# A hybrid layer in fp32: more groups of the two FFNs by seven products, sums of weights held in the program's place, loads asked for sooner

## The chip, the cores and the metric

One core of a Trainium2 chip runs the whole layer. The time is the device time of one execution in microseconds; the kernel before was run three times. Its five instruction streams are TensorE (PE; its weight loads are listed as PEld), VectorE (DVE), ScalarE (ACT), GpSimd (POOL) and SyncE (SP), which only issues DMAs here.

## The reference

One layer, 256 rows of 2048 numbers, all fp32, d_ff = 5632:

```python
x = x + 0.5 * swiglu(rms_norm(x, ffn1_norm), ffn1_w_gate, ffn1_w_up, ffn1_w_down)
h = rms_norm(x, mix_norm)
proj = h @ w_in                                   # u | q | k | v
y_ssm = s5_mixer(u, ...)                          # complex diagonal recurrence, chunks of 64, then GLU
y_sb = stick_breaking_attention(q, k, v)
mixed = concat(rms_norm(y_ssm), rms_norm(y_sb))
x = x + mixed @ w_out
x = x + 0.5 * swiglu(rms_norm(x, ffn2_norm), ffn2_w_gate, ffn2_w_up, ffn2_w_down)
x = x + rms_norm((p @ w_ple_proj) * sigmoid(rms_norm(x, ple_norm) @ w_ple_gate))

def swiglu(h, w_gate, w_up, w_down):
    return (silu(h @ w_gate) * (h @ w_up)) @ w_down
```

## The kernel before

Every fp32 product is made of three matmuls with a reduced type (fp32r): an operand is split into a high part (`whi` of a weight, by ScalarE, L168) and a low part (`wlo = w - whi`, by VectorE, L171), and high times high, high times low and low times high are added up in PSUM. Activations lie as stationary tiles of 128 x 128 (`nhi`, `nlo`, in the second FFN also `hhi`, `hlo`), weights move, 512 columns a matmul. A tile of weights is 128 x 1024, two of 128 rows.

Gate and up of an FFN are computed in NF = 11 blocks of 512 columns. The inner dimension of 2048 is cut into 4 groups of 512 rows (1 MB of weights each). A plain group has 4 halves (two of gate, two of up), each of 12 matmuls of 128x512 (`gemm_half`, L286, L287, L291): 48 in all. A half needs one `whi` and one `wlo`.

A group can also be done by seven products (`pair`; a scheme of Strassen's kind over gate and up together): the four quarters of weights of gate (`dg`) and up (`du`) and of activations are added and subtracted first, and seven products of 6 matmuls (`product`, L301, L305) take the place of the 48: 42 matmuls. The sums of weights are three `t` a group (L480, VectorE) and one more that a DMA adds in place (POOL's queue). The sums of activations (`shi`, `slo`) are made once by `quarter_sums` and kept. Behind the products of the first four kinds, four merges on VectorE (L516, L520, L523, L524; names `joined`, `left_over`, `parted`) and two copies on ScalarE move what is in one accumulator to the next; then the last three kinds of products are added. The remaining groups are plain (`rest`). In before the first FFN does two groups of blocks 7 to 10 in this way, the second two groups of blocks 1 to 10: 28 groups. With two groups there are 14 products: a0, a1, z0, z1, y0, y1, x0, x1, a'0, a'1, y'0, y'1, x'0, x'1 in the program's order.

When a block's up is complete, VectorE multiplies it with silu of gate (two instructions, `h`, L556 in a pair and L596 elsewhere), then turns the result for the down projection (`mid`, L203, 32 x 32 transpositions) and DMAs write it out (`hidden`). Then comes the next block's first product.

While the first FFN runs, the recurrence's constants are prepared in small pieces (`prep`, lines 860 to 990): a list `beside` holds generators, and `step()` advances each of them by one piece between halves of matmuls. The loads and sums of a pair (`fetch`), the delayed works (`put_off`) and the preparation are all such generators. The buffers of the pairs take the place of the preparation's, so the preparation has to be finished before the first pair's loads: `early = 6` in before.

The order on each engine: instructions that the program pins (`pin`) keep the program's order; the others are placed by a planner, by their costs and by what they need. Each engine then takes its instructions in the order laid down. Buffers that set the pace: four `whi`, four `wlo`, three `raw` (weights of 1 MB as loaded), four accumulators and two others (`aux`) in PSUM.

The norm ahead of an FFN (`Normed`) turns each block of 512 columns either on VectorE with 16 DMAs behind it (on a queue that is given), or, for the last blocks (`late`), by eight transposes on TensorE (L389).

Of the kernel before, what the change touches and what calls it, by code (L numbers as in the profile page):

```python
# [33 lines left out]
def layer_kernel(ctx: ExitStack, tc: tile.TileContext, a: dict, shapes: dict, out: bass.AP):  # L34
# [273 lines left out]

    def quarter_sums(pool, part):

        hi, lo = part
        full, s = (com("h").rearrange("p (j t) -> p j t", t=T), com("h").rearrange("p (i j t) -> p i j t", i=4, j=2))
        nc.vector.tensor_tensor(out=full, in0=hi.bitcast(F32), in1=lo.bitcast(F32), op=ALU.add)
        a11, a12, a21 = (full[:, 2 * k : 2 * k + 2, t * P : (t + 1) * P] for t, k in ((0, 0), (0, 1), (1, 0)))
        a22 = full[:, 2:, P:]
        for o, x, y, op in (
            (0, a21, a22, ALU.subtract), (1, s[:, 0], a11, ALU.subtract), (2, a11, a21, ALU.subtract),
            (3, a12, s[:, 1], ALU.add),
        ):
            nc.vector.tensor_tensor(out=s[:, o], in0=x, in1=y, op=op)  # L320
        shi, slo = (pool.tile([P, 4, 2, P], F32R, name=uid(n)) for n in ("shi", "slo"))
        split(shi, slo, s)
        quarters = [
            tuple(u[:, 2 * k : 2 * k + 2, t * P : (t + 1) * P] for u in part) for t, k in ((0, 0), (0, 1), (1, 1))
        ]
        return quarters, [(shi[:, i], slo[:, i]) for i in range(4)]

# [96 lines left out]

    def ffn(i, xn, nxt, bg=None):
        wg, wu, wd = (a[f"ffn{i}_w_{s}"][0] for s in ("gate", "up", "down"))
        hT = []
        pools = ExitStack()
        early = 6 if bg else NF
        hp = pools.enter_context(phase(f"h{i}"))  # L430
# [16 lines left out]

        first_pair = (early if bg else 0) + 1
        spare = "h" if bg else "n"
        left, right, sums, early_acts = [], {}, {}, {}  # L450
        n_groups = 2

        def fetch(f, steps=2):


            def g():
                todo = []
                for i in range(n_groups):
                    left_, right_ = (
                        get(hp, f"{s}{i}", 4 * NB).rearrange("p (j n) -> p j n", j=4) for s in ("dg", "du")  # L460
                    )
                    for d, w in ((left_, wg), (right_, wu)):
                        rows = w[i * NB : (i + 1) * NB, f * NB : (f + 1) * NB]
                        nc.sync.dma_start(d, rows.rearrange("(j p) n -> p j n", p=P))
                    t1, t2, t4 = (
                        (
                            actp.tile([P, 1024], F32, tag=spare + home, name=uid("t"), bufs={"n": 4, "h": 2}[spare])
                            if home
                            else get(hp, f"t{i}")
                        ).rearrange("p (j n) -> p j n", j=2)  # L470
                        for home in ("hi", "lo", "")
                    )
# [26 lines left out]

        def rest(ps, w, f):  # L500
            for k0 in range(4 * n_groups, KD, 4):
                part = xn(k0 // 4)
                for half in list(weight_halves(w, k0, 4, f * NB)):
                    end = k0 + 4 == KD and half[0] == 1
                    gemm_half(ps, (part, half), range(TT), False, end, skip_group_check=True)
                    step()

        def pair(f, prefetch):

            a, x, z, y = (acc() for _ in range(4))  # L510
            groups = [(*left[i], right.pop((f, i))) for i in range(n_groups)]
            c, u2 = get(hp, "c"), get(hp, "u2", NB)
            c1, c5 = c[:, :NB], c[:, NB:]

            def joined():
                nc.vector.tensor_tensor(out=u2, in0=z, in1=c1, op=ALU.add)  # L516

            def left_over():
                nc.scalar.copy(c5, y)
                nc.vector.tensor_tensor(out=y, in0=y, in1=u2, op=ALU.subtract)  # L520

            def parted():
                nc.vector.tensor_tensor(out=x, in0=x, in1=u2, op=ALU.add)  # L523
                nc.vector.tensor_tensor(out=z, in0=c5, in1=x, op=ALU.subtract)  # L524
# [10 lines left out]
            for i in range(len(todo)):  # L535
# [16 lines left out]
            rest([y, z], wu, f)  # L552
            hh = com("h")
# [5 lines left out]
            put_off(2, turned, hp, f, hh)  # L559

        for f in range(NF):
            if prep and f == min(early, NF - 1):
                finish(prep)
                side.close()
                prep = None
                hp = pools.enter_context(phase(f"h{i}b"))
            if f >= first_pair:
# [20 lines left out]
            if f + 1 == first_pair:  # L588
                left += [quarter_sums(hp, xn(i)) for i in range(n_groups)]
                fetch(f + 1, 1)  # L590
            pu = gemm_block(xn, wu, f * NB, KD)
# [13 lines left out]
    def down(w, hT, nxt, early_acts):  # L605
# [47 lines left out]
        def right(pool, g, n0):  # L653
# [9 lines left out]
            def g_():  # L663
                yield
                yield
                nc.vector.tensor_tensor(out=t, in0=b[2], in1=b[0], op=ALU.subtract)
                yield
# [117 lines left out]
    def s5_prep(pools):  # L785
# [82 lines left out]
        def cmul(o, x, mr, mi, shape, conj=False):  # L868
# [5 lines left out]
            for v, (u, m) in zip(tv, ((x[0], mrb), (x[1], mib), (x[1], mrb), (x[0], mib))):  # L874
                tt(out=v, in0=u, in1=m, op=ALU.mult)
            tt(out=o[0], in0=tv[0], in1=tv[1], op=ALU.add if conj else ALU.subtract)
# [52 lines left out]
        for q in range(NQ):  # L929
            r8 = slice(8 * q, 8 * q + 8)  # L930
# [3 lines left out]
            nc.scalar.dma_start(ceq[:, : 2 * P], a["ssm_c_laid"][:, q * 2 * P : (q + 1) * 2 * P])  # L934
            yield
# [11 lines left out]
            for i in range(2):  # L947
# [3 lines left out]
                for g in range(2):  # L951
                    sl = slice(64 * g, 64 * g + 64)
                    nc.scalar.copy(vv[sl, :, :, g, :], dvv[sl, :, i, :, :])
                    for b in range(2):
                        cv = cb[i][b].rearrange("p (r k g h) -> p k r g h", r=4, k=SL + 1, g=2)
                        nc.scalar.copy(cv[sl, :, :, g, :], cev[sl, :, i, 4 * b : 4 * b + 4, :])
            yield
            for i, n in enumerate(("m1r", "m1i")):
# [26 lines left out]
            mv = m3.rearrange("p (b r c) -> p b r c", b=2, r=4)  # L985
            for r in range(4):
                for sidx in range(SL):
                    o = mv[32 * sidx : 32 * sidx + 32, :, r, 32 * sidx :]
                    i = pv[32 * r : 32 * r + 32, :, : P - 32 * sidx]
                    nc.scalar.copy(o, i)  # L990
            nc.scalar.dma_start(scr["m3"][q], m3)
            yield


# [351 lines left out]

    n1, nm, n2, npl = Normed("ffn1_norm", load_turned), Normed("mix_norm"), Normed("ffn2_norm", kinds="hhnn", late=2), Normed("ple_norm")
    ffn(1, n1, nm, s5_prep)
# [31 lines left out]
    w_out = a["w_out"][0]  # L1380
    for n, side in ((0, 0), (1, 0), (0, 1), (1, 1), (2, 0), (2, 1), (3, 0), (3, 1)):
# [6 lines left out]
        if side:  # L1388
            put_off(2, n2.block, n)
    atp.close()  # L1390
    mix.close()

    ffn(2, n2, npl)


# [159 lines left out]
```

## Time and profile before

| | |
|---|---|
| Median of three runs (lowest, highest) | 1862.11 us (1862.07, 1864.48) |
| The profiled execution, its span | 1862.27 us, 1860.5 us |
| Granted TensorE clock | 0.999 |
| TensorE busy, VectorE, ScalarE, GpSimd | 99%, 80%, 59%, 4% |
| Mean DMA rate | 237 GB/s |

A profile row has the time of the start (in the timeline), the busy time, the engine, the line of the kernel, the operation, and the tile written and those read. What stands in brackets is the idle time of the engine just ahead and what ended it. In a table of stretches the columns are the stretch, its length, the busy time of PE, PEld, DVE, ACT and POOL with the number of instructions, the granted clock, the DMA engines' share and GB/s. In a list of waits: engine, tile and line that waited, what it waited for, us in total, times, the longest. A matmul's duration overlaps that of the next; the distance of two starts tells what one costs.

### The profile page before, as it was taken

Reading aid. Unit: us, or ns where it says so; the run is one execution under the profiler, and the core shown is the slowest. Engines: PE = TensorE matmul, PEld = TensorE weight load, DVE = VectorE, ACT = ScalarE, POOL = GpSimd, SP = SyncE. Lnnn points to the kernel's source line nnn. Section 1 sums busy time; section 2 is a strip of 40 time slices with the busy share of each in tenths; the row PEclk is TensorE's granted clock in tenths of the full one; section 3 lists DMA queues with packets and bytes.
Section 4 is the critical chain, followed back from the end, with each engine's and each line's share of the span. In section 5 each row is a group of like instructions: output and inputs, shape, how many; then the busy total and the mean of one; then the engine's idle time right before and its main releaser. Section 6 shows DMA issues by size and latency. Waiting matters only on the chain. (4 is left out here: it accounts for less than half of the span.)

```text
span 1860.5 us, 24329 instructions
## 1 busy us (share of the span) xinstructions
PE 1846.4 (99%) x8914; PEld 1522.4 (82%) x8914; DVE 1481.4 (80%) x1954; ACT 1103.6 (59%) x1343; POOL 72.2 (4%) x108
## 2 busy tenths in 40 slices
PE   9999999999999999999999999999999999999998
PEld 7888887888887888888898888888888888788886
DVE  8995767899877988686556879999889987798755
ACT  7456665566555665455785656556566655466654
POOL 0000000000000002010010000000000000000100
PEclk9999999999999999999999999999999999999999
DMA  8787779666888768675547757878677688775753
GB/s 320 228 263 248 260 248 308 232 226 215 290 255 279 222 199 304 226 259 184 204 137 242 255 153 246 269 239 264 215 243 227 224 296 262 258 240 194 233 198 125
DMA packets 272793, 441.40 MB, mean 237 GB/s; under 512 B 18208, under 2 KB 89120, under 8 KB 272544
## 3 DMA queue, kind: packets, MB, share of 16 engines
q1 hardware_dynamic: 254992, 409.06, 65.3%
q0 software_dynamic: 5056, 15.73, 4.2%
q10 hardware_dynamic: 12624, 15.04, 2.3%
q8 instruction: 70, 1.15, 0.3%
q14 instruction: 51, 0.42, 0.1%
HBM read 393.64 MB, written 26.21 MB: 226 GB/s over the span
## 5 line engine op out<-in xcount | busy, mean ns | idle before, releaser
L168 ACT CAST whi<-raw 128x1024 fp32r<-128x1024 f32 x514 | 535.8, 1052 | 467.4 <-PE acc L287 321.1
L171 DVE TENSOR_TENSOR wlo<-raw,whi 128x1024 fp32r<-128x1024 f32 x514 | 620.5, 1224 | 220.8 <-ACT whi L168 218.9
L286 PE MATMUL acc<-whi,nhi 128*128 128x512 f32 x1440 | 565.1, 392 | 2.5 <-ACT whi L168 2.3
L287 PE MATMUL acc<-whi,nlo 128*128 128x512 f32 x1440 | 561.2, 390 | 0.0
L291 PE MATMUL acc<-wlo,nhi 128*128 128x512 f32 x1440 | 386.4, 389 | 0.0
L286 PEld LDWEIGHTS acc<-whi,nhi 128*128 128x128 f32 x1440 | 270.6, 188 | 62.3 <-ACT whi L168 3.6
L291 PEld LDWEIGHTS acc<-wlo,nhi 128*128 128x128 f32 x1440 | 270.3, 188 | 56.4
L287 PEld LDWEIGHTS acc<-whi,nlo 128*128 128x128 f32 x1440 | 270.7, 188 | 55.1
L286 PE MATMUL acc<-whi,hhi 128*128 128x512 f32 x576 | 225.3, 391 | 0.0
L287 PE MATMUL acc<-whi,hlo 128*128 128x512 f32 x576 | 224.6, 390 | 0.0
L168 ACT CAST whi<-t 128x1024 fp32r<-128x1024 f32 x114 | 120.0, 1053 | 91.9 <-PE acc L287 52.2
L171 DVE TENSOR_TENSOR wlo<-t,whi 128x1024 fp32r<-128x1024 f32 x114 | 135.4, 1219 | 27.6 <-ACT whi L168 27.6
L291 PE MATMUL acc<-wlo,hhi 128*128 128x512 f32 x576 | 154.4, 390 | 2.9 <-DVE wlo L171 2.9
L291 PEld LDWEIGHTS acc<-wlo,hhi 128*128 128x128 f32 x576 | 107.8, 188 | 26.8 <-DVE wlo L171 4.6
L286 PEld LDWEIGHTS acc<-whi,hhi 128*128 128x128 f32 x576 | 108.2, 188 | 24.2
L287 PEld LDWEIGHTS acc<-whi,hlo 128*128 128x128 f32 x576 | 108.1, 188 | 23.2
L301 PE MATMUL acc<-whi,shi 128*128 128x512 f32 x224 | 89.2, 398 | 0.0
L301 PE MATMUL acc<-whi,slo 128*128 128x512 f32 x224 | 88.0, 393 | 0.0
L168 ACT CAST whi<-dg 128x1024 fp32r<-128x1024 f32 x56 | 58.6, 1050 | 30.4 <-PE acc L287 19.0
L171 DVE TENSOR_TENSOR wlo<-dg,whi 128x1024 fp32r<-128x1024 f32 x56 | 67.5, 1209 | 11.0 <-ACT whi L168 10.6
L305 PE MATMUL acc<-wlo,shi 128*128 128x512 f32 x224 | 70.4, 395 | 0.0
L171 DVE TENSOR_TENSOR wlo<-du,whi 128x1024 fp32r<-128x1024 f32 x56 | 67.6, 1207 | 0.0
(320 smaller groups left out, 2092.7 us busy)
## 6 DMA issues: line engine op xcount, KB each, us to landing
raw<-in_ffn_w_down SPq DMA_DIRECT2D x68, 1024.0 KB, 7.0
raw<-in_ffn_w_up SPq DMA_DIRECT2D x60, 1024.0 KB, 7.0
raw<-in_ffn_w_gate SPq DMA_DIRECT2D x58, 1024.0 KB, 7.3
raw<-in_w_in SPq DMA_DIRECT2D x32, 1024.0 KB, 5.6
dg<-in_ffn_w_gate SPq DMA_DIRECT2D x28, 1024.0 KB, 7.1
du<-in_ffn_w_up SPq DMA_DIRECT2D x28, 1024.0 KB, 8.9
hf<-hidden SPq DMA_DIRECT2D x44, 512.0 KB, 5.7
raw<-in_w_out SPq DMA_DIRECT2D x16, 1024.0 KB, 5.5
```

Of the source, the lines that this page charges most:

```text
L168: copy = nc.scalar.copy(hi, src)
L171: nc.vector.tensor_tensor(out=lo, in0=src, in1=hi.bitcast(F32), op=ALU.subtract)
L286: nc.tensor.matmul(ps[t], lhsT=lh, rhs=hi[:, j, cols], start=t in starts and j == 0, stop=False, **kw)
L287: nc.tensor.matmul(ps[t], lhsT=ll, rhs=hi[:, j, cols], start=False, stop=False, **kw)
L291: nc.tensor.matmul(ps[t], lhsT=lh, rhs=lo[:, j, cols], start=False, stop=stop and j == 1, **kw)
L301: nc.tensor.matmul(ps, lhsT=l[:, j], rhs=hi[:, j], start=start and i + j == 0, stop=False, skip_group_check=True)
L305: nc.tensor.matmul(ps, lhsT=ahi[:, j], rhs=lo[:, j], start=False, stop=j == 1, skip_group_check=True)
```

## The change

It does eight things.

1. `first_pair` of the first FFN is 4 instead of 7, with one group in blocks 4 to 7 and two in 8 to 10; of the second it is 0 instead of 1, with one group in block 0. 31 groups instead of 28.
2. The preparation ends at block 7 (`early = 7`) and is held while products run (`step(prep)`); 16 copies at the end of each of its stages become a generator of their own (`placed`), and its inputs are loaded a stage sooner (`inputs`).
3. The loads for the first pair (`fetch`) are spread (`gap=2`) and begin earlier.
4. The sums of weights are pinned (L487), and so is the addition of high and low parts in `quarter_sums` (L313) and a product in the preparation.
5. `u2` goes, its value being put in the place of `c1`.
6. `quarter_sums` works in place, and the sums of group 1 are made a block before they are needed.
7. The second FFN's norm turns all four blocks on VectorE (`late=0`), the third block's 16 DMAs on SP's queue, the fourth's on POOL's. The last four steps of the projection ahead of it are handed in as `lead`, so that the first pair's loads and sums go between them.
8. In block 0 of the second FFN the groups 1 and 2 of gate and of up come first, then group 3 of both.

On VectorE the program now has in block 3 of the second FFN the first of the following pieces in place of the second. `wlo` is a low part, `h` the product of silu and up of the block before, `t`, `tlo`, `thi` are sums of weights, `dg` and `du` weights as loaded. Of the change:

```order
L487 TENSOR_TENSOR tlo_1788_10284<-thi_1787_10283,du_1786_10280 128x1024
L487 TENSOR_TENSOR t_1784_10278<-tlo_1783_10277,dg_1780_10272 128x1024
L171 TENSOR_TENSOR wlo_10435<-dg_1780_10272,whi_10434 128x1024
L570 SCALAR_TENSOR_TENSOR h_10426<-acc_10098,sm_9491,sg_10334 128x512
L570 SCALAR_TENSOR_TENSOR h_10426<-acc_10099,sm_9491,sg_10334 128x512
L171 TENSOR_TENSOR wlo_10439<-dg_1785_10279,whi_10438 128x1024
L171 TENSOR_TENSOR wlo_10443<-tlo_1783_10277,whi_10442 128x1024
L171 TENSOR_TENSOR wlo_10453<-tlo_1788_10284,whi_10452 128x1024
L487 TENSOR_TENSOR t_1789_10285<-tlo_1788_10284,dg_1785_10279 128x1024
L171 TENSOR_TENSOR wlo_10465<-thi_1782_10276,whi_10464 128x1024
L171 TENSOR_TENSOR wlo_10475<-thi_1787_10283,whi_10474 128x1024
L523 TENSOR_TENSOR c_10433<-acc_10431,c_10433 128x512
```

Of before:

```order
L480 TENSOR_TENSOR t_1766_10206<-t_10205,dg_1762_10200 128x1024
L171 TENSOR_TENSOR wlo_10306<-raw_10303,whi_10305 128x1024
L171 TENSOR_TENSOR wlo_10310<-raw_10303,whi_10309 128x1024
L171 TENSOR_TENSOR wlo_10357<-dg_1757_10193,whi_10356 128x1024
L171 TENSOR_TENSOR wlo_10361<-dg_1762_10200,whi_10360 128x1024
L171 TENSOR_TENSOR wlo_10365<-t_10198,whi_10364 128x1024
L556 SCALAR_TENSOR_TENSOR h_10347<-acc_10019,sm_9456,sg_10255 128x512
L556 SCALAR_TENSOR_TENSOR h_10347<-acc_10018,sm_9456,sg_10255 128x512
L171 TENSOR_TENSOR wlo_10375<-t_10205,whi_10374 128x1024
L171 TENSOR_TENSOR wlo_10387<-t_10197,whi_10386 128x1024
L171 TENSOR_TENSOR wlo_10397<-t_10204,whi_10396 128x1024
```

Three low parts of the pair stood ahead of `h`, now one; all six sums stood ahead, now one stands behind three low parts. The same holds for blocks 5, 7 and 9. In blocks 2, 4, 6, 8, 10 of the second FFN, and 10 of the first, three low parts stay ahead and one sum comes behind `h`; in block 9 of the first two stay ahead; blocks 8 of the first and 1 of the second are as before.

On TensorE the second half of the same pair's products now reads as follows (`acc_10429` is a and a', `acc_10430` x, `acc_10432` y):

```order
L301 MATMUL acc_10430<-whi_10495,slo_9516 128x512
L305 MATMUL acc_10430<-wlo_10496,shi_9515 128x512 x2
L301 MATMUL acc_10432<-whi_10532,shi_9297 128x512
L301 MATMUL acc_10432<-whi_10532,slo_9298 128x512
L301 MATMUL acc_10432<-whi_10532,shi_9297 128x512
L301 MATMUL acc_10432<-whi_10532,slo_9298 128x512
L305 MATMUL acc_10429<-wlo_10511,hhi_9217 128x512 x2
L301 MATMUL acc_10429<-whi_10520,hhi_9325 128x512
...
L305 MATMUL acc_10429<-wlo_10521,hhi_9325 128x512 x2
L305 MATMUL acc_10432<-wlo_10533,shi_9297 128x512 x2
```

The low matmuls of the ninth product (`wlo_10511`) come behind its own four high ones, the rest of the eighth product and the high ones of y'; in before each product's six matmuls stand together.

On SP's queue the first pair's loads now stand among the plain loads of an earlier block:

```order
 L275 DMA raw_583<-in_ffn_w_gate 128x4x512
 L275 DMA raw_658<-in_ffn_w_gate 128x4x512
+L469 DMA dg_227_1520<-in_ffn_w_gate 128x4x512
 L275 DMA raw_719<-in_ffn_w_gate 128x4x512
 L133 DMA h_559<-in_not_ahead 128x128
+L469 DMA du_228_1521<-in_ffn_w_up 128x4x512
 L275 DMA raw_844<-in_ffn_w_up 128x4x512
 L275 DMA raw_923<-in_ffn_w_up 128x4x512
```

Two loads, each with a plain load behind it; in before four stood together.

The diff, cut to its core:

```diff
-    def step():
+    def step(but=None):
         for g in list(beside):
-            if next(g, beside) is beside:
+            if g is not but and next(g, beside) is beside:
...
-    def quarter_sums(pool, part):
+    def quarter_sums(pool, part, tag="h"):
...
+        full = com(tag).rearrange("p (j t) -> p j t", t=T)
+        pin(nc.vector.tensor_tensor(out=full, in0=hi.bitcast(F32), in1=lo.bitcast(F32), op=ALU.add))
...
-    def ffn(i, xn, nxt, bg=None):
+    def ffn(i, xn, nxt, bg=None, lead=()):
...
-        early = 6 if bg else NF
+        early = 7 if bg else NF
...
-        first_pair = (early if bg else 0) + 1
+        first_pair = 4 if bg else 0
+        homes = [hp, hp]
-        n_groups = 2
-        def fetch(f, steps=2):
+        def n_groups(f):
+            return 2 if f > (early if bg else 0) else 1
+        def fetch(f, steps=2, gap=0):
...
                         nc.sync.dma_start(d, rows.rearrange("(j p) n -> p j n", p=P))
+                        for _ in range(gap):
+                            yield
...
                     yield
-                    nc.vector.tensor_tensor(out=o, in0=x, in1=y, op=ALU.add)
+                    pin(nc.vector.tensor_tensor(out=o, in0=x, in1=y, op=ALU.add))
...
             def joined():
-                nc.vector.tensor_tensor(out=u2, in0=z, in1=c1, op=ALU.add)
+                nc.vector.tensor_tensor(out=c1, in0=z, in1=c1, op=ALU.add)
...
                 if i % 2 or i + 1 == len(todo):
-                    step()
+                    step(prep)
             finish(sums.pop(f))
...
-            rest([a, x], wg, f)
+            left_over_groups = list(range(n_groups(f), ND))
+            if len(left) < n_groups(f + 1):
+                left.append(quarter_sums(homes[1], xn(1), "sg"))
+            if f == 0:
+                rest([a, x], wg, f, left_over_groups[:-1])
+                rest([y, z], wu, f, left_over_groups[:-1])
+                del left_over_groups[:-1]
+            rest([a, x], wg, f, left_over_groups)
...
+        for n, block in enumerate(lead):
+            if n == 0:
+                fetch(0, 4, 2)
+            if n == len(lead) - 1:
+                left.append(quarter_sums(hp, xn(0), "sg"))
+            block()
...
+            if f + 1 == first_pair:
+                fetch(f + 1, 2, 2)
...
+            def placed(q=q, pv=pv, mv=mv):
+                for r in range(4):
+                    for sidx in range(SL):
...
+                        pin(nc.scalar.copy(o, i))
+                    yield
+                nc.scalar.dma_start(scr["m3"][q], m3)
+            last = start(placed())
...
-    n2 = Normed("ffn2_norm", kinds="hhnn", late=2)
+    n2 = Normed("ffn2_norm", kinds="hhnn", late=0)
...
+        if side and n == ND - 1:
+            put_off(0, n2.block, n, (1, 9), nc.gpsimd)
+        elif side:
+            put_off(1, n2.block, n, (3, 10), nc.sync)
...
+    blocks = [lambda n=n, side=side: project(n, side) for n in range(2, ND) for side in range(2)]
+    ffn(2, n2, npl, lead=blocks)
```

More of the change, by code (lines that the diff above doesn't have):

```diff
@@ L307, in product, with quarter @@
         return run
-    def quarter_sums(pool, part):
+    def quarter_sums(pool, part, tag="h"):
         hi, lo = part
[L312 to L315, printed above, removed]
+        full = com(tag).rearrange("p (j t) -> p j t", t=T)
+        pin(nc.vector.tensor_tensor(out=full, in0=hi.bitcast(F32), in1=lo.bitcast(F32), op=ALU.add))
+        def quarter(u, t, k):
+            return u[:, 2 * k : 2 * k + 2, t * P : (t + 1) * P]
+        a11, a12, a21, a22 = (quarter(full, t, k) for t in range(2) for k in range(2))
         for o, x, y, op in (
-            (0, a21, a22, ALU.subtract), (1, s[:, 0], a11, ALU.subtract), (2, a11, a21, ALU.subtract),
-            (3, a12, s[:, 1], ALU.add),
-        ):
[L320 to L326, printed above, removed]
+            (a22, a21, a22, ALU.subtract), (a21, a11, a21, ALU.subtract), (a11, a22, a11, ALU.subtract),
+            (a12, a12, a11, ALU.add),
+        ):
+            nc.vector.tensor_tensor(out=o, in0=x, in1=y, op=op)
+        sums = tuple(pool.tile([P, 4, T], F32R, name=uid(n)) for n in ("shi", "slo"))
+        split(*sums, full)
+        return (
+            [tuple(quarter(u, t, k) for u in part) for t, k in ((0, 0), (0, 1), (1, 1))],
+            [tuple(quarter(u, t, k) for u in sums) for t, k in ((1, 1), (0, 0), (1, 0), (0, 1))],
+        )
     def gemm_block(act, w, n0, nkt, first=()):
@@ L464, in g @@
                         nc.sync.dma_start(d, rows.rearrange("(j p) n -> p j n", p=P))
+                        for _ in range(gap):
+                            yield
                     t1, t2, t4 = (
                         (
-                            actp.tile([P, 1024], F32, tag=spare + home, name=uid("t"), bufs={"n": 4, "h": 2}[spare])
-                            if home
-                            else get(hp, f"t{i}")
+                            actp.tile([P, 1024], F32, tag="h" + home, name=uid("t"), bufs=2)
+                            if bg and home
+                            else get(homes[i], f"t{home}{i}")
                         ).rearrange("p (j n) -> p j n", j=2)
@@ L498, in begin_down, with rest @@
             put_off(5, halved)
[L500 to L504, printed above, removed]
+        def rest(ps, w, f, groups):
+            for g in groups:
+                part = xn(g)
+                for half in list(weight_halves(w, 4 * g, 4, f * NB)):
+                    end = g == ND - 1 and half[0] == 1
                     gemm_half(ps, (part, half), range(TT), False, end, skip_group_check=True)
@@ L510, in pair @@
             a, x, z, y = (acc() for _ in range(4))
-            groups = [(*left[i], right.pop((f, i))) for i in range(n_groups)]
-            c, u2 = get(hp, "c"), get(hp, "u2", NB)
+            groups = [(*left[i], right.pop((f, i))) for i in range(n_groups(f))]
+            c = get(hp, "c")
             c1, c5 = c[:, :NB], c[:, NB:]
             def joined():
-                nc.vector.tensor_tensor(out=u2, in0=z, in1=c1, op=ALU.add)
+                nc.vector.tensor_tensor(out=c1, in0=z, in1=c1, op=ALU.add)
             def left_over():
                 nc.scalar.copy(c5, y)
-                nc.vector.tensor_tensor(out=y, in0=y, in1=u2, op=ALU.subtract)
+                nc.vector.tensor_tensor(out=y, in0=y, in1=c1, op=ALU.subtract)
             def parted():
-                nc.vector.tensor_tensor(out=x, in0=x, in1=u2, op=ALU.add)
+                nc.vector.tensor_tensor(out=x, in0=x, in1=c1, op=ALU.add)
                 nc.vector.tensor_tensor(out=z, in0=c5, in1=x, op=ALU.subtract)
@@ L588, in ffn @@
             if f + 1 == first_pair:
-                left += [quarter_sums(hp, xn(i)) for i in range(n_groups)]
-                fetch(f + 1, 1)
+                left.append(quarter_sums(hp, xn(0)))
             pu = gemm_block(xn, wu, f * NB, KD)
@@ L663, in g_ @@
             def g_():
-                yield
-                yield
-                nc.vector.tensor_tensor(out=t, in0=b[2], in1=b[0], op=ALU.subtract)
+                for _ in range(4):
+                    yield
+                pin(nc.vector.tensor_tensor(out=t, in0=b[2], in1=b[0], op=ALU.subtract))
                 yield
@@ L927, in view, with inputs @@
             return [u[:, (2 * k + i) * P : (2 * k + i + 1) * P].rearrange("p (r h) -> p r h", h=HC) for i in range(2)]
-        for q in range(NQ):
-            r8 = slice(8 * q, 8 * q + 8)
+        def inputs(q):
             dv = get(sub, "dv")
@@ L934, in s5_prep @@
             nc.scalar.dma_start(ceq[:, : 2 * P], a["ssm_c_laid"][:, q * 2 * P : (q + 1) * 2 * P])
+            return dv
+        nxt_dv = inputs(0)
+        for q in range(NQ):
+            r8 = slice(8 * q, 8 * q + 8)
+            dv = nxt_dv
             yield
@@ L956, in s5_prep @@
                         nc.scalar.copy(cv[sl, :, :, g, :], cev[sl, :, i, 4 * b : 4 * b + 4, :])
+            if q + 1 < NQ:
+                nxt_dv = inputs(q + 1)
             yield
@@ L985, in s5_prep @@
             mv = m3.rearrange("p (b r c) -> p b r c", b=2, r=4)
[L986 to L991, printed above, removed]
+            def placed(q=q, pv=pv, mv=mv):
+                for r in range(4):
+                    for sidx in range(SL):
+                        o = mv[32 * sidx : 32 * sidx + 32, :, r, 32 * sidx :]
+                        i = pv[32 * r : 32 * r + 32, :, : P - 32 * sidx]
+                        pin(nc.scalar.copy(o, i))
+                    yield
+                nc.scalar.dma_start(scr["m3"][q], m3)
+            last = start(placed())
             yield
+        finish(last)
     ua = [None, None]
@@ L1380, in layer_kernel, with project @@
     w_out = a["w_out"][0]
-    for n, side in ((0, 0), (1, 0), (0, 1), (1, 1), (2, 0), (2, 1), (3, 0), (3, 1)):
+    def project(n, side):
         y, r = ((yss, rss), (ysb, rsb))[side]
@@ L1387, in layer_kernel @@
             )
-        if side:
-            put_off(2, n2.block, n)
+        if side and n == ND - 1:
+            put_off(0, n2.block, n, (1, 9), nc.gpsimd)
+        elif side:
+            put_off(1, n2.block, n, (3, 10), nc.sync)
+    for n, side in ((0, 0), (1, 0), (0, 1), (1, 1)):
+        project(n, side)
     atp.close()
     mix.close()
-    ffn(2, n2, npl)
+    blocks = [lambda n=n, side=side: project(n, side) for n in range(2, ND) for side in range(2)]
+    ffn(2, n2, npl, lead=blocks)
     fin = ctx.enter_context(phase("ple"))
```

13 lines of the change are left out of this document (6 added, 7 removed).

## The prediction

> **What bounds the kernel now.** I read the page's first part first, then the groups by line, then the waits, and last the order of time around the blocks that change.
>
> ```profile
> PE 1846.4 (99%) x8914; PEld 1522.4 (82%) x8914; DVE 1481.4 (80%) x1954; ACT 1103.6 (59%) x1343; POOL 72.2 (4%) x108
> PE acc L291 <- DVE wlo L171: 2.9, 4, 1.3
> PE acc L286 <- ACT whi L168: 2.3, 3, 1.5
> ```
>
> TensorE is busy 99% of a span of 1860.5 us, and its waits for the two engines that split the weights come to 5.2 us in all. So a matmul taken out counts in full, and a wait put in counts in full; there is no third place to hide. Busy time of a pipelined matmul overlaps the next one's, so I take starts, not durations. These rows of TensorE's timeline are a half of a plain group, then the first and the last product of a pair of groups, and what follows it:
>
> ```profile
> 1091.61 0.39 PE L286 MATMUL acc<-whi,nhi 128*128 128x512 f32 x1
> ...
> 1094.33 0.39 PE L286 MATMUL acc<-whi,nhi 128*128 128x512 f32 x1
> ...
> 1102.49 0.39 PE L301 MATMUL acc<-whi,hhi 128*128 128x512 f32 x1
> ...
> 1103.85 0.39 PE L301 MATMUL acc<-whi,hhi 128*128 128x512 f32 x1
> ...
> 1105.21 0.40 PE L301 MATMUL acc<-whi,shi 128*128 128x512 f32 x1
> ...
> 1106.61 0.40 PE L301 MATMUL acc<-whi,shi 128*128 128x512 f32 x1
> ...
> 1121.45 0.61 PE L305 MATMUL acc<-wlo,hhi 128*128 128x512 f32 x2
> 1121.90 0.39 PE L286 MATMUL acc<-whi,nhi 128*128 128x512 f32 x1
> ```
>
> A half (12 matmuls) takes 1094.33 - 1091.61 = 2.72 us, so a plain group of gate and up (4 halves) takes 10.88 us. Fourteen products take 1121.90 - 1102.49 = 19.41 us, so seven take 9.71 us: 1.36 us where the stationary tile is a quarter of the activations, 1.40 us where it is a sum of quarters. A group by seven products is worth 10.88 - 9.71 = 1.17 us.
>
> VectorE, at 80%, is the engine to fear: each block of a pair gives it most of a block's time. This is its timeline through one pair of before.
>
> ```profile
> 1100.15 1.22 DVE L171 TENSOR_TENSOR wlo<-t,whi 128x1024 fp32r<-128x1024 f32 x1 [1.50 <-ACT whi L168]
> 1102.46 1.41 DVE L596 SCALAR_TENSOR_TENSOR h<-acc,sm,sg 128x512 f32<-128x512 f32 x2 [1.09 <-PE acc L291]
> 1103.79 3.48 DVE L171 TENSOR_TENSOR wlo<-t,whi 128x1024 fp32r<-128x1024 f32 x3
> 1107.19 0.70 DVE L203 STREAM_TRANSPOSE mid<-h 128x512 f32<-128x512 f32 x1
> 1107.82 1.18 DVE L171 TENSOR_TENSOR wlo<-du,whi 128x1024 fp32r<-128x1024 f32 x1
> 1108.93 0.68 DVE L516 TENSOR_TENSOR u<-acc,c 128x512 f32<-128x512 f32 x1
> 1109.53 1.21 DVE L171 TENSOR_TENSOR wlo<-du,whi 128x1024 fp32r<-128x1024 f32 x1
> ...
> 1116.44 1.22 DVE L171 TENSOR_TENSOR wlo<-du,whi 128x1024 fp32r<-128x1024 f32 x1
> 1117.58 2.35 DVE L171 TENSOR_TENSOR wlo<-t,whi 128x1024 fp32r<-128x1024 f32 x2
> ```
>
> The reader is to see that VectorE stands still for 1.09 us in front of the two products h (the last matmul of up has to end first, 0.03 us before the first product starts), and has three low parts of the new pair ready by then. From there it runs without a gap: h twice 1.33 us, a low part 3.40 / 3 = 1.13 us a step, a transposition 0.63, a merge 0.60. The low part that is used at 1118.69 (twelfth product) is ready at 1116.44 + 1.22 = 1117.66: a lead of 1.0 us, the smallest of the pair. That lead is all the room that VectorE has in a pair.
>
> **The change part by part.** (The profiled execution is 1862.27 us, 0.16 above the median of the three runs; the sum is made on it.)
>
> *Products for plain groups.* First FFN: blocks 4, 5, 6 get one group each, block 7 goes from two to one; second FFN: block 0 gets one. Net three groups more, 3 x 1.17 = 3.5 us less, with 18 matmuls fewer.
>
> *No transposes by TensorE for the second norm's blocks 2 and 3.*
>
> ```profile
> 1043.58 1.03 PE L389 MATMUL aux<-ident,x 128*128 128x128 f32 x8
> 1044.37 0.47 PE L286 MATMUL acc<-whi,nhi 128*128 128x512 f32 x1
> 1044.68 0.39 PE L287 MATMUL acc<-whi,nlo 128*128 128x512 f32 x1
> ```
>
> Eight take 0.79 us and the first matmul behind them 0.31 instead of 0.23: 0.9 us, twice: 1.8 us less. In their place stand four transpositions on VectorE at 0.63 us and 32 small copies, 16 on SP's queue and 16 on POOL's. Sixteen of that kind on POOL, in before:
>
> ```profile
> 708.02 3.25 POOL L217 DMA_DIRECT2D h<-mid  x6 [268.17 <-DVE mid L203]
> ...
> 718.98 0.53 POOL L217 DMA_DIRECT2D h<-mid  x1 [0.99 <-DMA h<-mid]
> ```
>
> are issued over 11.5 us. Block 3's are wanted only by the last group of block 0, which the change puts behind the plain groups 1 and 2 of gate and of up, four times 5.44 us after the products; I take this at nothing. If that cover were too short, TensorE would wait up to the difference, a few us, once.
>
> *Loads of the first pair.* In before its four blocks of 1 MB are issued in one go at the end of block 5, and weights behind them come late:
>
> ```profile
> 292.41 0.37 SPq L464 DMA_DIRECT2D dg<-in_ffn_w_gate  x1
> ...
> 293.92 0.79 SPq L464 DMA_DIRECT2D du<-in_ffn_w_up  x1
> 316.21 2.00 ACT L168 CAST whi<-raw 128x1024 fp32r<-128x1024 f32 x2 [5.28 <-DMA raw<-in_ffn_w_up]
> 308.57 1.07 PE L291 MATMUL acc<-wlo,nhi 128*128 128x512 f32 x4
> 310.04 0.50 PE L286 MATMUL acc<-whi,nhi 128*128 128x512 f32 x1 [0.40 <-ACT whi L168]
> ...
> 314.74 1.07 PE L291 MATMUL acc<-wlo,nhi 128*128 128x512 f32 x4
> 317.30 0.50 PE L286 MATMUL acc<-whi,nhi 128*128 128x512 f32 x1 [1.49 <-ACT whi L168]
> 300.00:310.00 10.00, 9.64 (x43) 7.66 (x41) 8.60 (x8) 2.34 (x4) 1.94 (x2) 1.00 1.06 355
> 310.00:320.00 10.00, 8.47 (x36) 6.67 (x37) 4.72 (x4) 2.93 (x3) 0.00 (x0) 1.00 1.03 310
> ```
>
> The DMA share is over 1.0 there. Four matmuls of L291 take 0.91 us, so 310.04 - 308.57 holds 0.56 lost and 317.30 - 314.74 holds 1.65; with 0.3 for the slower matmuls right behind each, 2.5 us. After the change the first pair loads 2 MB, earlier, with a plain load between: I take the 2.5 us as gone (bounds: none of it, all of it).
>
> *Gains together:* 3.5 + 1.8 + 2.5 = 7.8, so 1854.5 us if nothing is added.
>
> *The pinned sums.* The sums of weight quarters (L480, now L487) keep the program's place, and the two h stand between others than before. In blocks 3, 5, 7, 9 of the second FFN only one low part stands ahead of the two h, and one sum stands behind them. VectorE takes its instructions in their order; a low part behind h waits for up's last matmul even where its inputs are there. So 2 + 1 steps of 1.13, 3.4 us, move behind the moment from which the lead of 1.0 us counts. Step by step, from the start of h: h, h 1.33; three low parts 3.40; the sum 1.13; two low parts 2.27; merge 0.60; two low parts 2.27; merge 0.60; two transpositions 1.26; the low part of the ninth product 1.13: ready at 14.0 us. TensorE's new order reaches it after eight whole products (2 x 1.36 + 6 x 1.40 = 11.1) and the eight high matmuls of two more (1.85): 13.0. It waits 1.05. Behind it VectorE makes a low part, a merge, a low part (2.9): 16.9; TensorE comes there 8 matmuls (1.85) after 14.05: 15.9. It waits another 1.0. Together 2.1 us a block, 8.4 us in four. By the rows alone the bounds are 0 (the lost steps find room that I don't see) and 3.4 - 1.0 = 2.4 a block; I take 2.1, by TensorE's own new order.
>
> [...]
>
> In blocks 2, 4, 6, 8, 10 three low parts stay ahead and one sum stands behind: 1.13 against a lead of 1.0, and TensorE's order has other work there: nothing, at most 0.1 each. Block 9 of the first FFN has two low parts ahead and a sum behind: 2.3 - 1.0 = 1.3 at most, 1.0 by TensorE's order. Block 7 of the first FFN: VectorE forms the next group's sums of quarters (L313) in front of the low part that the following plain half needs, one step of 1.13 with no lead left: 0 to 1.2, I take 0.6. Block 0 of the second: the fourth accumulator's merge comes last and the product into it is early: 0 to 0.9, I take 0.45. In blocks 4 to 6 of the first the seven low parts and three sums of a pair stand against four low parts of a plain group, 6 x 1.13 = 6.8 us more of VectorE a block; there this row shows it idle a third of the time, so nothing:
>
> ```profile
> 176.00:220.00 44.00, 44.00 (x228) 35.79 (x228) 28.51 (x68) 25.76 (x43) 0.00 (x0) 1.00 0.78 244
> ```
>
> The 16 copies on ACT that became a work beside lie in ACT's idle time, 40% here; the in-place c1 changes no count.
>
> *Sum:* 1862.27 - 7.8 + 8.4 + 1.0 + 0.6 + 0.45 = 1864.9; I say 1865.
>
> **The rivals.**
>
> *The waits don't come; the gains stay.* VectorE is idle 1.09 us ahead of h and 1.5 us ahead of the low parts before it, about 4 us a block, so per block it has room for the 3.4 us. Against it: that room lies ahead of h, and the order puts the steps behind. Were the waits a tenth of my sum, the time is 1854.5 + 1.0 = 1855.5; with a third of them 1858.
>
> *The burst of loads moves on and is paid as well.* With one group in block 7, block 8 is the first with two, and 4 MB for it are asked for in one go behind block 7's products, beside the writes of the hidden rows. That is the burst that cost 2.5 us; the 2.5 would then not be gained: 1865 + 2.5 = 1867.5, slower than before. It decides if the DMA share there passes 1.0 for some 10 us. Against it: in before each later pair asks for the same 4 MB and no wait is in these stretches:
>
> ```profile
> 348.00:391.00 43.00, 43.00 (x190) 35.31 (x189) 38.87 (x39) 25.70 (x28) 1.73 (x2) 1.00 0.71 240
> ```
>
> *The change doesn't do what it says*, the products of blocks 4 to 7 finding the recurrence's preparation still in their way on VectorE: then its 2.3 us of products and the 2.5 us of loads are lost, 1865 + 4.8 = 1869.8. The preparation is held while products run, so I give it little.
>
> **How the numbers follow.** A difference of 0.2%, 3.7 us, is about what a measurement of this kernel tells from none: faster is below 1858.4, slower above 1865.8. The forecast (waits about as worked out, 1861 to 1868) has a chance of 0.54: its centre lies 0.9 below the bound, so 0.34 of it falls to no change and 0.20 to slower. The gains alone, 1854.5 to 1859: 0.28, of which 0.26 faster. The burst: 0.13, 0.11 of it slower. The last: 0.05, slower 0.03. So faster 0.26, no change 0.40, slower 0.34. The range of 8 in 10 reaches from the first rival, 1855, to the page's and the burst's end, 1868.5; the likeliest case alone has 1861 to 1868.
>
> **What would show it.** In the changed kernel's profile: TensorE's waits for wlo (L171) should rise from 2.9 to some 11 us, in blocks 3, 5, 7 and 9 of the second FFN two waits of about 1 us each, on the low parts of the ninth and eleventh products, and none in 2, 4, 6, 8, 10. The waits for whi near 310 and 317 should be gone, and no transposes of L389's kind should stand between the projection's halves. If TensorE's waits for wlo stay under 3 us, the forecast is wrong and the first rival right; if waits for a raw load stand around block 8 of the first FFN, the second; if VectorE's gaps in front of h have closed in blocks 4 to 7, the third.

## The result: 1883.2 us, slower by 1.1%

The changed kernel takes 1883.2 us (median of 4 runs, 1882.01 to 1885.05), the kernel before, run beside it, 1862.09. The ratio is 1.0113, with a 95% interval of 1.0100 to 1.0126. The prediction was 1865 us and no change, with a range up to 1868.5: 18 us too low. The profiles below are of single executions, 1885.05 us after and 1862.27 before, so their spans lie 22.7 us apart where the medians lie 21.1 apart.

The first part of the page in the profile after (busy time, share of the span, instructions):

```profile
PE 1848.2 (98%) x8880; PEld 1512.9 (80%) x8880; DVE 1509.3 (80%) x1992; ACT 1114.6 (59%) x1360; POOL 83.5 (4%) x127
```

TensorE's waits in it (what waited, for what, us in total, times, the longest):

```profile
PE acc L305 <- DVE wlo L171: 8.0, 10, 1.0
PE acc L286 <- ACT whi L168: 5.1, 4, 2.5
PE acc L301 <- DVE h L570: 3.8, 2, 1.9
PE acc L301 <- DVE acc L527: 2.8, 3, 1.9
PE acc L291 <- DVE wlo L171: 2.4, 2, 1.5
PE acc L301 <- DVE slo L171: 1.1, 1, 1.1
```

There are 34 instructions of TensorE fewer (18 matmuls and 16 transposes), as there should be, but the waits for the other engines have grown, and two sorts are new: for `h` and for the merges (`acc`, L527) in front of a product.

Where the time went is best seen by blocks. The end of up's last matmul of each block was read from TensorE's timelines (start of that matmul and 0.23 us); the differences are the table, and a block's time below is the distance of two such ends.

| stretch | before, us | after, us | difference | the prediction's sum |
|---|---|---|---|---|
| first FFN, blocks 0 to 3 | 185.1 | 185.5 | +0.3 | 0 |
| blocks 4, 5, 6 | 143.2 | 148.4 | +5.2 | -6.0 |
| blocks 7 to 10 | 164.7 | 169.4 | +4.7 | +2.8 |
| first down projection, mixer, second FFN's block 0 | 609.5 | 610.5 | +1.0 | -2.5 |
| second FFN, blocks 1 to 10 | 411.7 | 425.7 | +14.0 | +8.4 |
| second down projection to the end | 346.3 | 343.8 | -2.5 | 0 |
| span | 1860.5 | 1883.2 | +22.7 | +2.7 |

(The prediction's column: products and loads in blocks 4 to 6, -3.5 and -2.5; one group less in block 7, 1.2, and the waits of blocks 7 and 9, 1.6; transposes, block 0's products and its wait, -1.8, -1.2 and +0.45; the pinned sums, 8.4.)

**The second FFN.** This is VectorE's timeline after the change through block 3's pair, and TensorE's at the two waits:

```profile
1196.57 1.41 DVE L570 SCALAR_TENSOR_TENSOR h<-acc,sm,sg 128x512 f32<-128x512 f32 x2 [3.04 <-PE acc L291]
1197.90 1.22 DVE L171 TENSOR_TENSOR wlo<-dg,whi 128x1024 fp32r<-128x1024 f32 x1
1199.03 2.35 DVE L171 TENSOR_TENSOR wlo<-tlo,whi 128x1024 fp32r<-128x1024 f32 x2
1201.30 1.22 DVE L487 TENSOR_TENSOR t<-tlo,dg 128x1024 f32<-128x1024 f32 x1
...
1208.17 1.29 DVE L203 STREAM_TRANSPOSE mid<-h 128x512 f32<-128x512 f32 x2
1209.39 2.32 DVE L171 TENSOR_TENSOR wlo<-dg,whi 128x1024 fp32r<-128x1024 f32 x2
1210.63 0.73 PE L305 MATMUL acc<-wlo,hhi 128*128 128x512 f32 x2 [0.99 <-DVE wlo L171]
1213.50 0.50 PE L305 MATMUL acc<-wlo,shi 128*128 128x512 f32 x1 [0.76 <-DVE wlo L171]
```

VectorE now stands still for 3.04 us in front of `h` (1.09 before), and from there on runs without a gap, with the sum (L487) among the low parts. The ninth product's low part is ready at 1209.39 + 1.22 = 1210.6, 14.0 us after h began, as worked out, and TensorE waits for it and again for the eleventh. Start to start the two places lose 1.16 and 0.91 us. The same stands in blocks 5, 7 and 9; each of the four takes 43.6 us instead of 41.2. Block 4 has a wait of another kind, for the high part of a plain load that came late:

```profile
1277.56 2.00 ACT L168 CAST whi<-raw 128x1024 fp32r<-128x1024 f32 x2 [5.78 <-DMA raw<-in_ffn_w_up]
1278.66 0.50 PE L286 MATMUL acc<-whi,nhi 128*128 128x512 f32 x1 [2.52 <-ACT whi L168]
```

**Blocks 4 to 6.** VectorE and ScalarE around the products of block 6, the start of its first product being at 283.2, and TensorE's wait:

```profile
282.41 0.89 DVE L896 TENSOR_TENSOR cm<-dv,s5s 128x128 f32<-128x128 f32 x4
...
283.63 1.22 DVE L171 TENSOR_TENSOR wlo<-t,whi 128x1024 fp32r<-128x1024 f32 x1
284.76 0.89 DVE L896 TENSOR_TENSOR cm<-dv,s5s 128x128 f32<-128x128 f32 x4
...
285.98 1.21 DVE L171 TENSOR_TENSOR wlo<-t,whi 128x1024 fp32r<-128x1024 f32 x1
287.11 1.40 DVE L570 SCALAR_TENSOR_TENSOR h<-acc,sm,sg 128x512 f32<-128x512 f32 x2
285.89 1.25 ACT L979 COPY vb<-dv 64x512 f32<-64x512 f32 x2 [2.75 <-DVE dv L897]
287.16 1.04 ACT L168 CAST whi<-du 128x1024 fp32r<-128x1024 f32 x1
288.23 1.18 ACT L1020 COPY m<-aux 32x256 f32<-32x256 f32 x4
288.00 0.47 PE L301 MATMUL acc<-whi,shi 128*128 128x512 f32 x1 [1.87 <-DVE h L570]
```

The preparation is held while the products run, but instructions of it stand among them all the same: `cm` ahead of `h` on VectorE, `vb` and `m` ahead of high parts on ScalarE. By the order in which the program issues them, `cm` came just before the pair; `m` belongs to `placed`, a generator of its own that `step(prep)` does not hold; and `vb` came behind the pair and was moved forward by the planner. The third product goes into an accumulator that `h` has to read first, and `h` begins 3.9 us after the first product. A single group comes to that accumulator after two products, two groups only after four; that alone costs nothing, as the run e3 below shows. Blocks 5 and 6 take 51.2 and 50.6 us; before, plain, they took 48.0 and 48.2.

### The profile page after: what moved, and what is told of

The parts are those of the page before. It is cut to its first block, busy times and chain, and to the rows that moved or that the text cites. A ratio compares the mean times of both kernels' runs of the same rounds, so it can differ in the third digit from the quotient of the medians.

```text
span 1883.2 us, 24392 instructions
## 1 busy us (share of the span) xinstructions
PE 1848.2 (98%) x8880; PEld 1512.9 (80%) x8880; DVE 1509.3 (80%) x1992; ACT 1114.6 (59%) x1360; POOL 83.5 (4%) x127
## 3 DMA queue, kind: packets, MB, share of 16 engines
q8 instruction: 69, 1.13, 0.2%
## 4 chain that ended last, share of the span: by engine, by line
PE 84%; DVE 7%; DMA 3%; issue 2%; ACT 2%; SPq 0%; ACTq 0%; DVEq 0%
PE acc L286 22%; PE acc L287 22%; PE acc L291 22%; PE acc L301 8%; PE acc L305 4%; DVE wlo L171 4%; PE aux L301 2%; DMA raw<-in_ffn_w_up 1%; PE aux L305 1%; ACT whi L168 1%; DMA raw<-in_w_out 1%; DVE mid L203 1%; DMA scr_m1r<-m 1%; DMA scr_cpr<-cb 0%; DVE cm L896 0%
## 5 line engine op out<-in xcount | busy, mean ns | idle before, releaser
L168 ACT CAST whi<-raw 128x1024 fp32r<-128x1024 f32 x502 | 523.4, 1052 | 459.7 <-PE acc L287 299.8
L171 DVE TENSOR_TENSOR wlo<-raw,whi 128x1024 fp32r<-128x1024 f32 x502 | 604.4, 1224 | 235.9 <-ACT whi L168 235.0
L286 PE MATMUL acc<-whi,nhi 128*128 128x512 f32 x1408 | 552.5, 392 | 6.6 <-ACT whi L168 5.1
L287 PE MATMUL acc<-whi,nlo 128*128 128x512 f32 x1408 | 548.2, 390 | 0.0
L291 PE MATMUL acc<-wlo,nhi 128*128 128x512 f32 x1408 | 378.2, 389 | 2.4 <-DVE wlo L171 2.4
L168 ACT CAST whi<-t 128x1024 fp32r<-128x1024 f32 x81 | 84.9, 1051 | 65.1 <-PE acc L287 23.8
L171 DVE TENSOR_TENSOR wlo<-t,whi 128x1024 fp32r<-128x1024 f32 x81 | 97.1, 1218 | 17.8 <-ACT whi L168 17.7
L301 PE MATMUL acc<-whi,shi 128*128 128x512 f32 x248 | 98.9, 399 | 6.6 <-DVE h L570 3.8
L301 PE MATMUL acc<-whi,slo 128*128 128x512 f32 x248 | 97.8, 394 | 1.1 <-DVE slo L171 1.1
L305 PE MATMUL acc<-wlo,shi 128*128 128x512 f32 x248 | 79.6, 402 | 3.8 <-DVE wlo L171 3.8
```

The lines of the kernel that those rows point to most:

```text
L168: copy = nc.scalar.copy(hi, src)
L171: nc.vector.tensor_tensor(out=lo, in0=src, in1=hi.bitcast(F32), op=ALU.subtract)
L286: nc.tensor.matmul(ps[t], lhsT=lh, rhs=hi[:, j, cols], start=t in starts and j == 0, stop=False, **kw)
L287: nc.tensor.matmul(ps[t], lhsT=ll, rhs=hi[:, j, cols], start=False, stop=False, **kw)
L291: nc.tensor.matmul(ps[t], lhsT=lh, rhs=lo[:, j, cols], start=False, stop=stop and j == 1, **kw)
L301: nc.tensor.matmul(ps, lhsT=l[:, j], rhs=hi[:, j], start=start and i + j == 0, stop=False, skip_group_check=True)
```

## The experiments

Each kernel is the changed one with the edit shown, or the one before where that is said. The runs are called e1 to e7, in the order in which they were planned; what an expectation calls the fifth run is e5.

### Is it the pin?

```diff
-                    pin(nc.vector.tensor_tensor(out=o, in0=x, in1=y, op=ALU.add))
+                    nc.vector.tensor_tensor(out=o, in0=x, in1=y, op=ALU.add)
```

> The changed kernel with the sums of weights (L487) no longer held in the program's place; all else of the change stays. Theory A (the pin puts the last sum behind h and low parts behind h with it): the two waits of 0.9 and 1.2 us in each of blocks 3, 5, 7 and 9 of the second FFN go, a block there takes 41.2 us instead of 43.4, blocks 2, 4, 6, 8, 10 lose their 0.5 us, block 9 of the first its 1.0: 12 to 15 us less than the changed kernel, 1868 to 1871. Rival B (the in-place c1, which the next merge has to read before it is written again, or the later loads, hold the products up): within 2 us of the changed kernel, 1883.

Measured (e1): 1866.02 us (10 runs; ratio to before 1.0023, interval 1.0013 to 1.0032), 17 us less than the changed kernel. The second FFN's blocks 1 to 10 take 412.2 us instead of 425.7, 41.2 each but for one with 41.6, and no wait is left there (the list of TensorE's waits is empty from 1115 to 1522 us). Theory A holds, B falls. Beyond what was expected it gave 2.7 us at the start of the second FFN, where the pinned sums had stood ahead of the last steps of the projection, 2.4 in the first FFN (1.0 of it expected), and in block 4 of the second a wait of 2.5 us for a late load went with it.

```diff
-                fetch(f + 1)
+                fetch(f + 1, 1)
```

> The changed kernel, the sums still pinned, but the loads of a pair wait one step instead of two before the sums begin, so that the sixth sum falls ahead of h. Theory A: as good as without the pin to about 1 us, 1869 to 1873, because only one low part more than before stands behind h (1.13 us against a lead of 1.0). Rival C (pinning as such costs, by holding other instructions on VectorE back): 1880 or more.

Measured (e2): 1869.91 us, one run. Pinned, but a step sooner, the sums cost almost nothing in the blocks: blocks 3, 5, 7, 9 take 41.4 or 41.5 us (one low part of 1.13 more behind h, where the lead was 1.0), the others 41.2. So in the blocks it isn't pinning as such that costs, it is where the sixth sum stands in the program: the generator that makes them advances once a half, the two plain groups have eight halves, and with two steps of waiting the sixth sum falls into the next block's products. Before, the planner moved it forward and hid that. At the start of the second FFN, which this edit doesn't touch, the pin itself still costs: the stretch from the first FFN to block 0 of the second takes 611.8 us here and 610.5 in the changed kernel, but 607.8 in e1. That is about the whole of the 4 us between e1 and e2.

```diff
-                    nc.vector.tensor_tensor(out=o, in0=x, in1=y, op=ALU.add)
+                    pin(nc.vector.tensor_tensor(out=o, in0=x, in1=y, op=ALU.add))
```

on the kernel before, nothing else:

> The kernel before with one edit: its sums of weights (L480) pinned. Theory A, by the blocks of the changed kernel (2.25 us where one low part stands ahead of h and a sum behind, 0.5 where three stand ahead and a sum behind): five blocks of the first sort (block 9 of the first FFN, blocks 3, 5, 7, 9 of the second) and seven of the second sort, 11.2 + 3.5 = 14.7 us more than before, 1876; two waits of about 1 us in each of the five. Rival B (only together with the in-place c1): 1862 to 1865.

Measured (e6): 1870.88 us, one run, 9 more than before, not 14.7. The blocks lose what was expected: 3.2 us in blocks 7 to 10 of the first FFN (41.4, 41.4, 43.6, 41.4), 11.1 in blocks 1 to 10 of the second, with ten waits for low parts:

```profile
PE acc L305 <- DVE wlo L171: 8.8, 10, 1.0
```

B falls again. What is missing is a gain elsewhere: TensorE's four waits in the down projections are gone in this kernel too, 2.0 and 2.3 us less in those stretches, and block 6 of the first FFN took 1.5 less in this execution.

### Is it the preparation?

```diff
             if prep and f == 0:
                 start(prep)
+                start(prep)
```

> The changed kernel with the recurrence's preparation advanced two pieces a step, so that all of it lies in blocks 0 to 3 and none in blocks 4 to 6 of the first FFN. Theory D (the waits in blocks 4 to 6 come from the preparation's pieces that stand in ScalarE's and VectorE's order in front of the split of a product's weights and of h): blocks 4, 5 and 6, which take 49.3, 51.1 and 48.5 us, take 42.4 to 43.0 each, the seven products of a single group without a wait over 0.5 us; blocks 1 to 3 become longer by the preparation's TensorE work and by its own waits. Rival E (a single group's products wait for each other's merges on VectorE whatever stands beside): waits of 0.7 to 2 us stay in blocks 4 to 6, which take 44.5 us or more.

Measured (e3): 1903.02 us, one run; blocks 4, 5 and 6 take 42.4 us each, and TensorE waits for nothing from 227 to 354 us. Theory D holds, E falls. (The expectation counts from the start of one `h` to the next; by the ends of up, the three blocks of the changed kernel take 46.6, 51.2 and 50.6 us.) The same place in block 6 in this run:

```profile
310.37 1.41 DVE L570 SCALAR_TENSOR_TENSOR h<-acc,sm,sg 128x512 f32<-128x512 f32 x2 [1.09 <-PE acc L291]
311.69 1.22 DVE L171 TENSOR_TENSOR wlo<-du,whi 128x1024 fp32r<-128x1024 f32 x1
```

h begins as soon as up's last matmul is done and nothing is in its way. A plain block is four groups, 43.5 us; 42.4 is 43.5 less 1.17: the products' gain is all there. The kernel as a whole is slower because the same pieces, two a step, now crowd blocks 2 and 3 (64.8 and 65.3 us), so this is no remedy.

```diff
-        early = 7 if bg else NF
+        early = 6 if bg else NF
-        first_pair = 4 if bg else 0
+        first_pair = 7 if bg else 0
-                left.append(quarter_sums(hp, xn(0)))
+                left += [quarter_sums(homes[1], xn(i)) for i in range(n_groups(first_pair))]
```

and the sums unpinned as in e1:

> The changed kernel with the sums unpinned and with the first FFN's groups as before: two groups of blocks 7 to 10 by products, plain blocks 4 to 6, preparation finished at block 6; the loads of the first pair still sooner and spread, the rest of the change stays. Theory D (blocks 4 to 6 lose more by the preparation in their way than their products save): with the sums unpinned block 10 of the first FFN was done at 502.2 us, before at 494.4; this kernel is done there at 492 to 495, and takes 7 to 10 us less than the 1866.0 of the unpinned one, 1856 to 1859, below the kernel before. Rival H (the new pieces of the preparation, its inputs and its 16 copies as a work beside, cost the time wherever the pairs stand): block 10 at 500 or later, 1864 or more.

Measured (e5): 1855.44 us (6 runs), a ratio of 0.9966 to before, interval 0.9954 to 0.9978: faster than both kernels, by 6.3 us than the one before, and a little below what D expected. Up of block 10 of the first FFN is done at 490.6 us, and its two `h`, which the expectation counts, at 492.0. D holds, H falls. The list of TensorE's waits is short now, and begins:

```profile
PE aux L1517 <- ACT diag L1516: 2.7, 1, 2.7
PE aux L228 <- POOL ones L126: 1.1, 1, 1.1
PE acc L286 <- ACT whi L168: 0.7, 2, 0.4
PE acc L301 <- DVE sm L413: 0.7, 1, 0.7
```

The first FFN is 2.4 us shorter than before (in block 6, where the waits at 310 and 317 us are gone, the first pair's loads being asked for sooner), the stretch from there to the second FFN's block 0 2.5, the end 2.4. These are readings of one profile each, and no run takes the parts of this gain one by one.

```diff
-        first_pair = 7 if bg else 0
+        first_pair = 6 if bg else 0
```

on the kernel of e5, with the sums of quarters of group 1 made behind the first plain group of block 6:

> The kernel of the fifth run with one group more by products: block 6 of the first FFN gets one, after the preparation's end at block 6, and the sums of quarters of group 1 are made behind the first plain group of its gate. Theory D (a single group's products pay where no piece of the preparation stands between them): block 6 takes 1.2 us less, 1854.3, unless the preparation's last pieces, which are all put in at block 6, stand in ScalarE's and VectorE's order in front of a product. Rival E (a single group has no slack between its products): a wait of 0.5 to 2 us in block 6, 1855 to 1857.

Measured (e7): 1857.61 us (11 runs; ratio to before 0.998, interval 0.9971 to 0.9989), 2 us more than without that group. Block 6 takes 47.1 us against 45.7 in e5, and 1.9 us more went at the second FFN's start, most of it in a wait of 2.3 us for a load of the projection. ScalarE's timeline in its products says why:

```profile
282.79 4.72 ACT L1024 COPY m<-aux 32x256 f32<-32x256 f32 x16 [0.44 <-DVE aux L1016]
287.53 0.59 ACT L535 COPY c<-acc 128x512 f32<-128x512 f32 x1
289.12 0.50 PE L301 MATMUL acc<-whi,nhi 128*128 128x512 f32 x1 [1.15 <-ACT whi L168]
```

The 16 copies of the preparation's last stage stand for 4.72 us in front of the pair's copy and its next high parts. That is D's exception, written ahead of the run. E's numbers would fit the time too; the row, and e3, decide for the preparation.

### The down projections' waits

TensorE's four waits there (0.31, 1.44, 0.43, 1.40 us start to start) are gone after the change. The edit tried here is part of the change, though the list of its eight parts leaves it out, and the prediction has no term for it. On the kernel before:

```diff
-                yield
-                yield
-                nc.vector.tensor_tensor(out=t, in0=b[2], in1=b[0], op=ALU.subtract)
+                for _ in range(4):
+                    yield
+                pin(nc.vector.tensor_tensor(out=t, in0=b[2], in1=b[0], op=ALU.subtract))
```

> The kernel before with one edit of the change alone: in the down projection the first sum of weights is pinned and comes two steps later. Theory F (this edit is why the four waits of TensorE in the two down projections, 0.31, 1.44, 0.43 and 1.40 us, are gone in the changed kernel): 3.6 us less than the kernel before, 1858.5, the four waits gone. Rival G (they are gone because other things come at other times): 1862, the waits still there.

Measured (e4): 1861.03 us (10 runs; ratio 0.9995, interval 0.9986 to 1.0005). In the profile the four waits are gone, and the two stretches are 2.0 and 1.7 us shorter, so the edit does it; but in that execution up of block 10 of the first FFN, whose code is the same, was done at 496.4 us instead of 493.0, and over all runs the gain of 3.6 isn't there: the interval leaves room for 2.6 at most. F is right about the place and wrong about the total; what took the gain away elsewhere is open. With e6 it is clear that another edit, the pin on the FFN's sums, takes the same waits away.

## Why the prediction was wrong, point by point

- *A group by seven products is worth 1.17 us, a matmul counts in full.* Right: 42.4 us for a block with one group (e3).
- *The pinned sums, 2.1 us a block in blocks 3, 5, 7 and 9.* Right in place, cause and size: 1.16 + 0.91 at the ninth and the eleventh product. Block 9 of the first FFN, forecast at 1.0, lost 1.1; block 7's wait behind the sums of quarters, forecast at 0.6, was 1.05, and 0.85 came in front of a product that waits for a merge (L531), which had no term.
- *Blocks 2, 4, 6, 8, 10: at most 0.1 each.* Mis-sized: 0.3 each, 1.4 us in all; blocks 3, 5, 7 and 9 lost 2.45 with the slower matmuls behind their waits (the two at 1210.63 take 0.57 us start to start, 0.45 where no wait stands ahead, as at 1069.12), 9.8 instead of 8.4. Beside that stands block 4's single wait of 2.5 us for a plain load that came late; it is not in the kernel without the pin. What made that load late was not tried by itself.
- *Blocks 4 to 6 of the first FFN: nothing, because VectorE is idle a third of the time there.* This is the step that failed, by 11 of the 20 us between the forecast difference of the spans and the measured one: -6.0 forecast, +5.2 measured. A mean share of idle time over 44 us said nothing about which instruction stands in front of `h` at the moment when TensorE needs its accumulator. The prediction counted VectorE's work and ScalarE's idle share, and did not read the order of the preparation's instructions there as it had for the sums. In the changed kernel VectorE is still idle a quarter of the time in blocks 4 to 6 (busy 112.6 us of 148.4), while TensorE waits for it. The prediction also left out that a single group comes two products sooner to an accumulator that waits for `h`. The loads' wait of 2.5 us at 310 and 317 did go, as forecast, and so did the products' 3.5; some 11 us of new waits, and of slower matmuls behind them, stood against that (in TensorE's list from 182 to 342 us 3.8 for `h`, 2.8 for merges and 1.5 for a high part; the first matmul behind such a wait took 0.31 to 0.34 us to the next start instead of 0.23).
- *That rival* (the preparation still in the way) had a price of 5 us, less than half of what came, and a chance of only 0.05, because the preparation was taken to be out of the way once it was held.
- *The second FFN's start, a loss of 0.45.* Mis-sized: five waits of 5.1 us in all between 1054 and 1081 us (start to start), two of them (1.6 and 1.3) behind the sums of quarters that VectorE had still to make:

```profile
1061.28 1.21 DVE L313 TENSOR_TENSOR sg<-hhi,hlo 128x1024 f32<-128x1024 f32 x1
1064.41 1.21 PE L291 MATMUL acc<-wlo,nhi 128*128 128x512 f32 x4 [1.47 <-DVE wlo L171]
1071.10 0.50 PE L301 MATMUL acc<-whi,slo 128*128 128x512 f32 x1 [1.13 <-DVE slo L171]
```

  Without the pin (e1) 2.5 us of waits are left, 1.2 of them in block 0, as much as its products gain.
- *The in-place c1 and the copies as a work beside, nothing.* The first holds, as far as e1 and e5 go. The second does not where products stand near (the 4.72 us in e7).
- *The down projections* were taken as unchanged; here the stretch from the second on is 2.5 us shorter, and 1.75 us of waits in the first are gone too.
- *The range's upper end, 1868.5.* The burst's sum ends at 1867.5. What lies above it stood for a step of VectorE longer than 1.13 us, and no run shows that term: in the changed kernel the step from one low part to the next is 1.13 us again (1197.90 to 1199.03).

## What to carry to other kernels

TensorE was busy 98 and 99% of the span here, and the order of the other engines decided; their share of idle time (VectorE's, a quarter of blocks 4 to 6) couldn't speak for it. So for each instruction that the busy engine waits for, list what stands ahead of it in its own queue. Before a pin is set, see which place the planner had given the instruction, for the pin takes away a repair that nobody had written down; one step in a generator was worth 13 us (1869.91 in e2 against 1883.2). The work that was held by not issuing more of it still had in the queues what it had issued before (`cm` at 282.41 and 284.76), and what the planner moved forward (`vb` at 285.89).

## What was not expected of the hardware

After one wait of about 2 us TensorE's matmuls ran at about half pace for a while. In e1, behind a wait of 1.89 us:

```profile
285.62 0.70 PE L301 MATMUL acc<-whi,shi 128*128 128x512 f32 x1 [1.89 <-DVE h L570]
286.12 0.63 PE L301 MATMUL acc<-whi,slo 128*128 128x512 f32 x1
286.54 0.63 PE L301 MATMUL acc<-whi,shi 128*128 128x512 f32 x1
286.97 0.63 PE L301 MATMUL acc<-whi,slo 128*128 128x512 f32 x1
287.40 1.05 PE L305 MATMUL acc<-wlo,shi 128*128 128x512 f32 x2
288.25 0.63 PE L301 MATMUL acc<-whi,shi 128*128 128x512 f32 x1
288.68 0.59 PE L301 MATMUL acc<-whi,slo 128*128 128x512 f32 x1
```

and in the table of stretches (the granted clock, 0.79, stands ahead of the DMA share):

```profile
282.00:290.00 8.00, 6.11 (x20) 4.57 (x19) 7.14 (x14) 6.35 (x11) 0.00 (x0) 0.79 0.16 66
```

Starts are 0.43 us apart instead of 0.23, and the granted clock of that stretch is 0.79; the nearly equal wait at 288.00 in the changed kernel had no such tail (0.31, then 0.23 us), and its wait of 2.52 us had none either (0.34, then 0.23 us behind 1278.66, a clock of 1.00 from 1274 to 1282 us). In e3, with more and longer waits (19.1 us in nine waits for high parts in the whole run, the longest 4.2), the clock was 0.92 over blocks 2 and 3, and 0.72 from 200 to 212 us, where starts were 0.42 to 0.43 us apart ahead of the wait of 4.22 us (from 200.45 us on) and again behind it (0.60, then 0.42 and 0.43). So the wait in e1 cost some 1.4 us more than its own length (the seven distances from 285.62 to 288.68 take 3.06 us, at 0.23 each 1.61), and the changed kernel's two some 0.1; what decides it these runs don't show. And one stretch of code, the first FFN of the kernel before, was done at 493.0 us in one execution and at 496.4 in another; a gain of 3 us there is not to be read from one profile, and the 2.4 us that e1 and e5 show in the first FFN are no larger than that.
